# Attention scores of two heads as products in halves of the TensorE array, in a one-core hybrid encoder block

## The chip, the cores and the metric

The kernel runs on one core of one Trainium2 chip. The metric is the device time of one execution in microseconds (us); the time of a kernel is the median of several executions. TensorE (PE) multiplies matrices, VectorE (DVE), ScalarE (ACT) and GpSimd (POOL) do the work by elements, and SyncE (SP) issues most of the DMAs. A product reads a stationary operand, which a weight load (PEld in the profile) puts into the array first, and a moving operand, and writes into PSUM, which the kernel divides into eight banks of 128 partitions by 512 float32.

## What is computed

One encoder block over 1024 tokens of width 1024, in float32 accuracy:

```
h = rms_norm(x); [q|k|v|u] = h @ w_in
A: 8 heads x 64: 2-D neighbourhood attention on a 16 x 64 grid of tokens,
   window 8 rows x 16 columns, per-head RMS norm of q and k, relative-position bias
B: 4 groups x 128: centred mean pooling (windows 2, 4, 8, 16) minus the token,
   a linear map per group, a scale per channel
x = x + concat(A, B) @ w_out
x = x + (silu(h2 @ w_gate) * (h2 @ w_up)) @ w_down,  h2 = rms_norm(x)
```

For each query, attention takes the 8 x 16 keys of its window: scores times 1/8 plus bias, softmax, and the sum of the values.

## The kernel before

Every large product is made of three products of float32r operands: an operand is split into a high part (h) and the rest (l), and h*h, h*l and l*h are added in PSUM. `split` makes the parts: ACT writes h, DVE the rest. Tokens are ordered so that a tile of 64 queries is 4 rows by 16 columns, and a block of 128 keys is 4 rows by 32 columns.

Three stages follow one another. First the input projection of head pair 0, and the pooling branch. Then, for the four head pairs p, a stage in which attention is threaded between dense products (the projections of the next pairs, then `w_out`). Last the SwiGLU with its products of sums of blocks. The change touches the second stage.

There a unit is (p, b, Q): head pair p, one of four column strips b, one of four query tiles Q. 64 units. For each unit:

- `scores` (L561): the 64 queries of both heads lie as a block-diagonal 128 x 128 stationary operand (`qbd`, rows of head 0 against queries of head 0, rows of head 1 against those of head 1, zero elsewhere), so the output has head 0 on 64 partitions and head 1 on the other 64. The keys of two or three blocks are the moving operand: 256 or 384 columns (`QR`). Three products go into the one bank of the pool `ssp`. DVE adds the (negated) bias `nb` and takes the minimum (L581), ACT takes the exponential with its sum (L592), DVE the reciprocal (L594), POOL multiplies in place (L595).
- `transposes` (L600), `LAG` = 2 units later: two or three PE transposes into one of the two banks of the pool `ptp`, then a split into `pthl`.
- `values` (L611), one unit later: for each block of keys R, three products of the values with all the query tiles that see it, added in the bank of the pool `pop`; after the last, two ACT copies into `mixf`.

`spread_q` (L544) writes the block-diagonal operand of a strip from `qf`, half of the partitions at a time: four ACT copies and four POOL subtractions per strip. `load_bias` (L535) fetches `nb` and negates it on POOL, three times per head pair. `proj_evac_b` (L294) transposes the normalised q and k into a bank of `ptp`; ACT writes scaled q (`qf`), and `split` writes `kh` and `kl`.

The order on PE is the program's order in this stage (`pin`). `step(u)` issues scores of unit u, transposes of unit u-2 and values of unit u-3, and then `run` takes some dense pieces (`FIRST`, `CYC`, `WCYC`), each of three products. A scheduler with its own estimate of times orders the other engines; each works its queue in order. A pool hands out its banks in turn, and an allocation waits until the bank's last reader is done. Large tiles come from 45 slots of 4 KB per partition (`slot`), with the same rule.

Of the kernel before, what the change touches and what calls it, by code (L numbers as in the profile page):

```python
# [30 lines left out]
QR = [[0, 1], [0, 1, 2], [1, 2, 3], [2, 3]]  # L31
RQ = [[0, 1], [0, 1, 2], [1, 2, 3], [2, 3]]
BCOL = [0, 256, 256, 640]
BW = 896
LAG = 2
# [19 lines left out]
def hybrid_block(ctx, tc, xT, xt, w1, wu, rpbx, wpool, wout, wgu, wd, g2, sm, out):  # L55
# [7 lines left out]
    ssp = ctx.enter_context(tc.tile_pool(name="ssp", bufs=1, space=PSUM))  # L63
    ptp = ctx.enter_context(tc.tile_pool(name="ptp", bufs=2, space=PSUM))
# [150 lines left out]
    def proj_alloc(p):  # L215
        qf = slot(F32, f"qf_{p}")
# [4 lines left out]
        kT[p], qT[p], vn[p] = (kh, kl), qf, (vnh, vnl)  # L221
        for a in (qf, kh, kl, vnh[:, 0], vnl[:, 0]):
            touch(a)
# [70 lines left out]
    def proj_evac_b(p, tt, pool=ptp):  # L294
        (kh, kl), qf = kT[p], qT[p]
# [25 lines left out]
    def u_pool(up, hook):  # L321
# [10 lines left out]
        for half in range(2):  # L332
            ps = bank(ssp, f"rb_{half}")
# [30 lines left out]
        def u_win(g):  # L364
# [38 lines left out]
            for half in range(2):  # L403
                ps = bank((ssp, pop)[half], f"py_{g}_{half}")
# [31 lines left out]
    sq_ = ExitStack()  # L436
    qp = sq_.enter_context(tc.tile_pool(name="qp", bufs=1))
    qbd = []
    for i in range(2):
        pair = []  # L440
        for s in "hl":
            q_ = qp.tile([P, 4, 2, 64], F32R, name=f"qbd{s}{i}")
            nc.gpsimd.memset(q_.bitcast(F32), 0.0)
            pair.append(q_)
        qbd.append(pair)
# [5 lines left out]
    ps = bank(ptp, "warm_ps")  # L451
# [30 lines left out]
    pj = [bank(pl, f"pj_0_{t}") for t, pl in enumerate((mmp, mmp, mmp, mmp, ssp, pop, ptp, ptp))]  # L482
# [23 lines left out]
    def turn(tt):  # L506
        proj_evac_b(0, tt, (mmp, mmp, pop, ptp)[tt])
# [27 lines left out]
    def load_bias(p, b):  # L535
# [3 lines left out]
        nb = ap.tile([P, BW], F32, name=f"nb_{p}_{b}", tag="nb", bufs=2)  # L539
# [4 lines left out]
    def spread_q(p, b):  # L544
        qv = qT[p].rearrange("p (q b i) -> p q b i", q=4, b=4)
        bh, bl = qbd[b % 2]
        for qs in (slice(0, 2), slice(2, 4)):
            for j in range(2):
                pr = slice(64 * j, 64 * j + 64)
                nc.scalar.copy(bh[pr, qs, j, :], qv[pr, qs, b, :])  # L550
                nc.gpsimd.tensor_tensor(  # L551
                    out=bl[pr, qs, j, :],
                    in0=qv[pr, qs, b, :],
                    in1=bh[pr, qs, j, :].bitcast(F32),
                    op=ALU.subtract,
                )

    units = [(p, b, Q) for p in range(NPAIR) for b in range(4) for Q in range(4)]
    es, pos = {}, {}

    def scores(p, b, Q):  # L561
        kh, kl = (a.rearrange("p (r n) -> p r n", n=256) for a in kT[p])
        bh, bl = qbd[b % 2]
        nb = nbs[p, b]
        c0 = CG0[b] * 32
        rs = QR[Q]
        n = len(rs) * P
        ps = bank(ssp, f"s_{p}_{b}_{Q}")
        rsl = slice(rs[0], rs[-1] + 1)
        mm3(  # L570
            ps[:, :n],
            bh[:, Q].rearrange("p j i -> p (j i)"),
            bl[:, Q].rearrange("p j i -> p (j i)"),
            kh[:, rsl, c0 : c0 + P],
            kl[:, rsl, c0 : c0 + P],
            True,
            True,
        )
        e = tp.tile([P, 384], F32, name=f"e_{p}_{b}_{Q}", tag="e", bufs=4)
        m = tp.tile([P, 1], F32, name=f"m_{p}_{b}_{Q}", tag="m")  # L580
        nc.vector.tensor_tensor_reduce(  # L581
            out=e[:, :n],
            in0=ps[:, :n],
            in1=nb[:, BCOL[Q] : BCOL[Q] + n],
            scale=1.0,
            scalar=BIG,
            op0=ALU.add,
            op1=ALU.min,
            accum_out=m,
        )  # L590
        sm = tp.tile([P, 1], F32, name=f"sm_{p}_{b}_{Q}", tag="sm")
        nc.scalar.activation(e[:, :n], e[:, :n], AF.Exp, bias=m, scale=-1.0, accum_out=sm)  # L592
        r = tp.tile([P, 1], F32, name=f"r_{p}_{b}_{Q}", tag="r")
        nc.vector.reciprocal(r, sm)  # L594
        nc.gpsimd.tensor_scalar(  # L595
            out=e[:, :n], in0=e[:, :n], scalar1=r, scalar2=1.0, op0=ALU.mult, op1=ALU.mult
        )
        es[p, b, Q] = e

    def transposes(p, b, Q):  # L600
        e = es.pop((p, b, Q))
        rs = QR[Q]
        n = len(rs) * P
        pt = bank(ptp, f"pt_{p}_{b}_{Q}")
        for i in range(len(rs)):
            tr(pt[:, i * P : i * P + P], e[:, i * P : i * P + P], ident)
        at = [0, 1, 4, 7][Q]
        sel = slice(at, at + 2 * len(rs) - 1, 2)
        split(pthl[0][:, sel, :], pthl[1][:, sel, :], pt[:, :n].rearrange("p (r i) -> p r i", i=P))

    def values(p, b, R):  # L611
# [3 lines left out]
        q0 = RQ[R][0]  # L615
        nq = len(RQ[R])
# [4 lines left out]
        dst = po[:, q0 * P : (q0 + nq) * P]  # L621
        base = [0, 2, 5, 8][R]
        ph, pl = (a[:, base : base + nq, :].rearrange("p a i -> p (a i)") for a in pthl)
# [3 lines left out]
        if R == 3:  # L627
            mv = mixf[p].rearrange("p (q b i) -> p q b i", q=4, b=4)
            pv = po.rearrange("p (q j i) -> p q j i", q=4, j=2)
            for j in range(2):  # L630
                pr = slice(64 * j, 64 * j + 64)
                nc.scalar.copy(mv[pr, :, b, :], pv[pr, :, j, :])

    def step(u):
        if u < len(units):
            p, b, Q = units[u]
            if b == 0 and Q == 0:
                attn_alloc(p)
            nxt = units[u + 4 - Q] if u + 4 - Q < len(units) else None
            if nxt and Q == 1:  # L640
                load_bias(*nxt[:2])
            if nxt and Q == 2:
                spread_q(*nxt[:2])
            scores(p, b, Q)
        if 0 <= u - LAG < len(units):
            transposes(*units[u - LAG])
        if 0 <= u - LAG - 1 < len(units):
            p, b, Q = units[u - LAG - 1]
            for R in ((), (0,), (1,), (2, 3))[Q]:
                values(p, b, R)  # L650

# [193 lines left out]
    pthl = [ap.tile([P, 10, P], F32R, name=f"pt_{h}") for h in "hl"]  # L845
    load_bias(0, 0)
    spread_q(0, 0)
    for u in range(len(units) + LAG + 1):
        if u % 16 == 14:
            flush()  # L850
        step(u)
# [6 lines left out]
        elif u > W0:  # L858
            run(WCYC[min(u - W0 - 1, len(WCYC) - 1)])
    run(1000)  # L860
    pin = False
    sa.close()
    sq_.close()
# [20 lines left out]
    banks2 = (ptp, ptp, pop)  # L884
# [218 lines left out]
    ring = (mmp, mmp, ssp, mmp, mmp)  # L1103
# [24 lines left out]
    sets = ((mmp, mmp, mmp, mmp), (ptp, ssp, ptp, pop))  # L1128
# [181 lines left out]
def _bias_layout(np, rpb):  # L1310
# [3 lines left out]
    j, cg, rq, c8 = p // 64, p // 32 % 2, p // 8 % 4, p % 8  # L1314
    out = np.empty((NPAIR, 3, P, BW), rpb.dtype)
    for b, pat in ((0, 0), (1, 1), (3, 2)):
        for Q in (0, 1, 3):
            rs = QR[Q]
            n = np.arange(len(rs) * P)
            key_row = (rs[0] + n // P) * 4 + n // 8 % 4  # L1320
            key_col = (CG0[b] + n // 32 % 4) * 8 + n % 8
            row, col = 4 * Q + rq, 16 * b + 8 * cg + c8
# [4 lines left out]
            for pr in range(NPAIR):  # L1327
                out[pr, pat, :, BCOL[Q] : BCOL[Q] + n.size] = pad[(2 * pr + j)[:, None], ri, ci]
# [45 lines left out]
```

## Time and profile before

| | before |
|---|---|
| median of 3 runs | 1023.52 us (1022.57 to 1025.68) |
| profiled execution: time, span | 1024.31 us, 1022.4 us |
| PE, weight loads (share of the span) | 99%, 85% |
| DVE, ACT, POOL | 63%, 42%, 39% |
| mean granted TensorE clock | 0.997 |
| attention stage | about 107 to 325 us |

Busy time says how long an engine had work, not that the work set the end. A row of the timeline gives start, duration, engine, line, operation, and out<-in. Products are pipelined, so that a product's duration in a row is longer than what it keeps PE from the next one; the distance between two starts is the second. In a row of groups, the figures after the bar are busy time in us and the mean ns of one.

### The profile page before, as it was taken

What the parts mean: (1) busy time and instruction counts of PE and PEld (TensorE: products, weight loads), DVE (VectorE), ACT (ScalarE), POOL (GpSimd) and SP (SyncE); (2) the same over time, 40 slices, a digit from 0 to 9 for tenths busy, and PEclk for the clock granted to TensorE, in tenths of its full rate; (3) what the DMA queues carried; (4) which work ended last, traced back from release to release, by engine and by line L of the source; (5) the groups of instructions that cost most, each with busy time, mean ns of one, the idle gap of its engine ahead of it and who ended that gap; (6) DMA issues with size and microseconds to landing.
All of it is one profiled execution on the core that took longest, in us unless ns stands there. A gap on an engine that the chain in (4) does not pass through costs nothing.

```text
span 1022.4 us, 13679 instructions
## 1 busy us (share of the span) xinstructions
PE 1007.9 (99%) x4905; PEld 866.5 (85%) x4905; DVE 648.6 (63%) x1115; ACT 429.5 (42%) x876; POOL 400.5 (39%) x448
## 2 busy tenths in 40 slices
PE   9899999999999998999999999999999999999998
PEld 9888999999788887888888888888888888888887
DVE  5577666668652667856545546545562499988872
ACT  7542676667842335523333233233241354533400
POOL 1000333344731145468648658657644400000180
PEclk9999999999999999999999999999999999999999
DMA  9400413134511323133133133233216984373402
GB/s 355 175 16 1 127 53 107 50 119 163 180 42 42 144 83 93 53 112 136 72 124 114 72 123 113 74 123 113 78 78 224 350 277 150 102 244 114 134 32 93
DMA packets 50117, 124.12 MB, mean 121 GB/s; under 512 B 5312, under 2 KB 14272, under 8 KB 50048
## 3 DMA queue, kind: packets, MB, share of 16 engines
q1 hardware_dynamic: 43120, 98.85, 29.0%
q0 software_dynamic: 5632, 20.19, 5.3%
q10 hardware_dynamic: 1296, 4.20, 1.0%
q8 instruction: 39, 0.64, 0.3%
q14 instruction: 30, 0.25, 0.1%
HBM read 90.45 MB, written 28.57 MB: 116 GB/s over the span
## 4 chain that ended last, share of the span: by engine, by line
PE 93%; DVE 4%; ACT 1%; issue 1%; DMA 1%; POOL 0%; ACTq 0%; DVEq 0%; SPq 0%; POOLq 0%
PE pj L89 12%; PE z L89 12%; PE w L89 12%; PE x L89 11%; PE pw L89 7%; PE pc L89 6%; PE pa L89 6%; PE y L89 6%; PE pd L89 6%; PE pu L89 4%; PE pb L89 3%; PE po L89 3%; PE s L89 3%; PE pt L94 2%; PE qkt L94 1%
## 5 line engine op out<-in xcount | busy, mean ns | idle before, releaser
L89 PE MATMUL x<-b_h,w 128*128 128x512 f32 x352 | 116.5, 393 | 0.0
L89 PE MATMUL pw<-wo,mx 128*128 128x512 f32 x384 | 94.2, 396 | 0.3 <-DVE vnl L279 0.2
L89 PE MATMUL pj<-w1h,xh 128*128 128x384 f32 x256 | 87.2, 346 | 0.0
L89 PE MATMUL pj<-w1l,xh 128*128 128x384 f32 x256 | 84.6, 335 | 0.0
L89 PE MATMUL pj<-w1h,xl 128*128 128x384 f32 x256 | 83.7, 336 | 0.0
L89 PEld LDWEIGHTS pw<-wo,mx 128*128 128x128 f32 x384 | 70.8, 189 | 14.6 <-DVE x L776 0.5
L1300 POOL TENSOR_TENSOR x2r<-x2r,u 128x512 f32<-128x512 f32 x12 | 23.8, 2024 | 149.7 <-DVE u L1258 149.7
L89 PEld LDWEIGHTS x<-b_h,w 128*128 128x128 f32 x352 | 66.3, 189 | 13.7
L595 POOL TENSOR_SCALAR e<-e,r 128x256 f32<-128x256 f32 (+1 forms) x64 | 39.5, 618 | 75.8 <-DVE r L594 75.1
L89 PE MATMUL x<-b_l,w 128*128 128x512 f32 x176 | 68.9, 391 | 0.0
L1019 POOL TENSOR_TENSOR ur<-ur,gr 128x512 f32<-128x512 f32 x33 | 52.8, 1601 | 39.7 <-issue 22.0
L116 DVE TENSOR_TENSOR w_s<-sa,w_s 128x512 fp32r<-128x512 f32 x44 | 45.5, 1034 | 27.8 <-ACT w_s L115 27.7
L115 ACT CAST a_h<-raw_a 128x1024 fp32r<-128x1024 f32 (+1 forms) x42 | 41.0, 978 | 48.9 <-PE pc L89 13.8
L89 PE MATMUL z<-bt_h,w_s 128*128 128x512 f32 x176 | 57.9, 389 | 0.0
L89 PE MATMUL w<-b_h,w_s 128*128 128x512 f32 x176 | 57.8, 389 | 0.0
L89 PE MATMUL z<-bt_h,w 128*128 128x512 f32 x176 | 57.8, 389 | 0.0
L89 PE MATMUL y<-bt_h,w_s 128*128 128x512 f32 x176 | 57.8, 389 | 0.0
L89 PE MATMUL w<-bt_h,w_s 128*128 128x512 f32 x176 | 57.8, 389 | 0.0
L551 POOL TENSOR_TENSOR qbdl<-qf,qbdh 64x128 fp32r<-64x128 f32 x64 | 30.1, 471 | 64.6 <-ACT qbdh L550 56.2
L581 DVE CUSTOM_DVE_ANT_0 e<-s,nb 128x256 f32<-128x256 f32 (+1 forms) x64 | 31.1, 486 | 33.7 <-PE s L89 32.9
L116 DVE TENSOR_TENSOR a_l<-raw_a,a_h 128x1024 fp32r<-128x1024 f32 (+1 forms) x42 | 49.8, 1189 | 3.4 <-ACT a_h L115 3.1
L972 POOL TENSOR_TENSOR sa<-raw_g,raw_g 128x512 f32<-128x512 f32 x11 | 14.7, 1341 | 94.0 <-DMA raw_g<-in_wgu 81.8
(256 smaller groups left out, 2804.2 us busy)
## 6 DMA issues: line engine op xcount, KB each, us to landing
raw_a<-gsd SPq DMA_DIRECT2D x77, 256.0 KB, 3.6
raw_g<-in_wgu SPq DMA_DIRECT2D x22, 512.0 KB, 4.1
raw_u<-in_wgu SPq DMA_DIRECT2D x22, 512.0 KB, 4.1
gsd<-gr POOLq DMA_DIRECT2D x22, 512.0 KB, 4.0
raw_d<-in_wd SPq DMA_DIRECT2D x20, 512.0 KB, 4.3
raw_w<-in_w SPq DMA_DIRECT2D x15, 384.0 KB, 4.1
gsd<-ur POOLq DMA_DIRECT2D x11, 512.0 KB, 3.2
nb<-in_rpbx SPq DMA_DIRECT2D x12, 448.0 KB, 3.8
```

The costliest lines, as they stand in the source:

```text
L89: i = nc.tensor.matmul(*a, **k)
L94: i = nc.tensor.transpose(*a)
L115: keep(nc.scalar.copy(h, src))
L116: keepd(nc.vector.tensor_tensor(out=l, in0=src, in1=h.bitcast(F32), op=ALU.subtract))
L551: nc.gpsimd.tensor_tensor(out=bl[pr, qs, j, :], in0=qv[pr, qs, b, :], in1=bh[pr, qs, j, :].bitcast(F32), op=ALU.subtract,)
L581: nc.vector.tensor_tensor_reduce(out=e[:, :n], in0=ps[:, :n], in1=nb[:, BCOL[Q] : BCOL[Q] + n], scale=1.0, scalar=BIG, op0=ALU.add, op1=AL ...
L595: nc.gpsimd.tensor_scalar(out=e[:, :n], in0=e[:, :n], scalar1=r, scalar2=1.0, op0=ALU.mult, op1=ALU.mult)
L972: tt(out=s1, in0=r0[:, 1], in1=r1[:, 1], op=ALU.add)
L1019: eng.tensor_tensor(out=res[i][c][:, l], in0=src, in1=g, op=ALU.mult)
L1300: nc.gpsimd.tensor_tensor(out=q, in0=q, in1=U2[c], op=ALU.add)
```

## The change

A unit becomes (p, b, H): two query tiles at a time, 32 units. No block-diagonal queries are made. Instead `proj_evac_b` splits q into `qh` and `ql`, and a product takes 64 partitions (one head) of them, with 128 queries as its stationary columns, against 64 partitions of the keys, always three blocks (384 columns). The six products of a unit alternate between the two heads, which lie on partitions 0 to 63 and 64 to 127, and write to two banks. Scores, transposes and the transposes of q and k share a pool of three banks (`stp`) in place of `ssp` and `ptp`. `LAG` is 1 (larger) unit, the values come ahead of the dense pieces and the transposes, and the dense pieces of two former units stand between them. `nb` has 2 x 2 x 384 columns instead of 896, and `pthl` is laid out by key block, head and query.

```diff
-LAG = 2
+LAG = 1
-    ssp = ctx.enter_context(tc.tile_pool(name="ssp", bufs=1, space=PSUM))
-    ptp = ctx.enter_context(tc.tile_pool(name="ptp", bufs=2, space=PSUM))
+    stp = ctx.enter_context(tc.tile_pool(name="stp", bufs=3, space=PSUM))
...
 def proj_evac_b(p, tt, pool=stp):
-        keep(nc.scalar.activation(qf[:, c], pt[:, 0:256], AF.Copy, scale=qscale))
+        qo = [a.rearrange("p (h b q i) -> p h q b i", h=2, b=4, q=2)[:, tt // 2, tt % 2] for a in (qh, ql)]
+        qi = pt[:, 0:256].rearrange("p (b i) -> p b i", b=4)
+        keep(nc.scalar.activation(qo[0], qi, AF.Copy, scale=qscale))
+        keepd(nc.vector.scalar_tensor_tensor(out=qo[1], in0=qi, scalar=qscale,
+              in1=qo[0].bitcast(F32), op0=ALU.mult, op1=ALU.subtract))
         split(kh[:, c], kl[:, c], pt[:, 256:512])
...
-        nb = ap.tile([P, BW], F32, name=f"nb_{p}_{b}", tag="nb", bufs=2)
+        nb = ap.tile([P, 2, 2, 384], F32, name=f"nb_{p}_{b}", tag="nb", bufs=2)
...
-    def spread_q(p, b):
...
+    units = [(p, b, H) for p in range(NPAIR) for b in range(4) for H in range(2)]
+    def scores(p, b, H):
+        heads = [slice(64 * j, 64 * j + 64) for j in range(2)]
+        pss = [bank(stp, f"s_{p}_{b}_{H}_{j}") for j in range(2)]
+        for n, (x, y) in enumerate(((0, 0), (0, 1), (1, 0))):
+            for ps, js in zip(pss, heads):
+                mm(ps[:, :384], qv[x][js, H, b], kv[y][js, H : H + 3, c0 : c0 + P],
+                   start=n == 0, stop=n == 2)
+        for j, ps in enumerate(pss):
+            e = tp.tile([P, 384], F32, name=f"e_{p}_{b}_{H}_{j}", tag="e", bufs=4)
+            nc.vector.tensor_tensor_reduce(out=e, in0=ps[:, :384], in1=nb[:, H, j], ...)
+            nc.scalar.activation(e, e, AF.Exp, bias=m, scale=-1.0, accum_out=sm[:, j : j + 1])
+        nc.vector.reciprocal(r, sm)
+        for j, e in enumerate(es[p, b, H]):
+            nc.gpsimd.tensor_scalar(out=e, in0=e, scalar1=r[:, j : j + 1], ...)
+    def transposes(p, b, H):
+        pts = [bank(stp, f"pt_{p}_{b}_{H}_{j}") for j in range(2)]
+        for e, pt in zip(es[p, b, H], pts):
+            for i in range(3):
+                tr(pt[:, i * P : i * P + P], e[:, i * P : i * P + P], ident)
+        for j, pt in enumerate(pts):
+            h, l = (a[:, H : H + 3, j, P * H : P * H + P] for a in pthl)
+            split(h, l, pt[:, :384].rearrange("p (r i) -> p r i", i=P))
+    def step(v, more):
+        ... load_bias of the next strip at H == 0; scores(v)
+        if 0 <= v - LAG - 1 < len(units):
+            p, b, H = units[v - LAG - 1]
+            for R in ((0,), (1, 2, 3))[H]:
+                values(p, b, R)
+        more(2 * v)
+        if 0 <= v - LAG < len(units):
+            transposes(*units[v - LAG])
+        more(2 * v + 1)
```

`more(u)` holds the former choice of dense pieces for unit u. The other users of `ssp` and `ptp` (the first projections, the pooling branch, the SwiGLU) take `stp` instead; `BCOL`, `BW`, `QR`, `qbd` and its pool are gone; the bias array is laid out anew on the host side of the call.

More of the change, by code (lines that the diff above doesn't have):

```diff
@@ L434, in cook_wu @@
         cook(("wu", g), *wus[g])
[L436 to L445, printed above, removed]
     su = ExitStack()
@@ L450, in hybrid_block @@
     nc.vector.memset(warm.bitcast(F32), 0.0)
-    ps = bank(ptp, "warm_ps")
+    ps = bank(stp, "warm_ps")
     for _ in range(WARM):
@@ L481, in hybrid_block @@
     cook_wu(0)
-    pj = [bank(pl, f"pj_0_{t}") for t, pl in enumerate((mmp, mmp, mmp, mmp, ssp, pop, ptp, ptp))]
+    pj = [bank(pl, f"pj_0_{t}") for t, pl in enumerate((mmp, mmp, mmp, mmp, stp, pop, stp, stp))]
     pin = True
@@ L542, in load_bias @@
         nbs[p, b] = nb
-    def spread_q(p, b):
[L545 to L556, printed above, removed]
@@ L558, in hybrid_block @@
-    units = [(p, b, Q) for p in range(NPAIR) for b in range(4) for Q in range(4)]
+    units = [(p, b, H) for p in range(NPAIR) for b in range(4) for H in range(2)]
     es, pos = {}, {}
-    def scores(p, b, Q):
-        kh, kl = (a.rearrange("p (r n) -> p r n", n=256) for a in kT[p])
-        bh, bl = qbd[b % 2]
+    def scores(p, b, H):
+        kv = [a.rearrange("p (r n) -> p r n", n=256) for a in kT[p]]
+        qv = [a.rearrange("p (h b n) -> p h b n", h=2, b=4) for a in qT[p]]
         nb = nbs[p, b]
@@ L581, in scores @@
[L581 to L609, printed above, removed]
+        heads = [slice(64 * j, 64 * j + 64) for j in range(2)]
@@ new lines, in scores @@
+        es[p, b, H] = []
+        for j, ps in enumerate(pss):
+            e = tp.tile([P, 384], F32, name=f"e_{p}_{b}_{H}_{j}", tag="e", bufs=4)
+            m = tp.tile([P, 1], F32, name=f"m_{p}_{b}_{H}_{j}", tag="m", bufs=4)
+            nc.vector.tensor_tensor_reduce(
+                out=e,
+                in0=ps[:, :384],
+                in1=nb[:, H, j],
+                scale=1.0,
+                scalar=BIG,
+                op0=ALU.add,
+                op1=ALU.min,
+                accum_out=m,
+            )
+            nc.scalar.activation(e, e, AF.Exp, bias=m, scale=-1.0, accum_out=sm[:, j : j + 1])
+            es[p, b, H].append(e)
@@ L628, in values @@
             mv = mixf[p].rearrange("p (q b i) -> p q b i", q=4, b=4)
-            pv = po.rearrange("p (q j i) -> p q j i", q=4, j=2)
             for j in range(2):
                 pr = slice(64 * j, 64 * j + 64)
[L632 to L637, printed above, removed]
-                attn_alloc(p)
[L639 to L649, printed above, removed]
+                nc.scalar.copy(mv[pr, :, b, :], pv[pr, j].rearrange("p (q i) -> p q i", q=4))
+    def step(v, more):
+        if v < len(units):
+            p, b, H = units[v]
+            if b == 0 and H == 0:
+                attn_alloc(p)
+            if H == 0 and v + 2 < len(units):
+                load_bias(*units[v + 2][:2])
+            scores(p, b, H)
+        if 0 <= v - LAG - 1 < len(units):
+            p, b, H = units[v - LAG - 1]
+            for R in ((0,), (1, 2, 3))[H]:
                 values(p, b, R)
+        more(2 * v)
+        if 0 <= v - LAG < len(units):
+            transposes(*units[v - LAG])
+        more(2 * v + 1)
     late = []
@@ L844, in hybrid_block, with more @@
     tp = sa.enter_context(tc.tile_pool(name="tp", bufs=3))
-    pthl = [ap.tile([P, 10, P], F32R, name=f"pt_{h}") for h in "hl"]
+    pthl = [ap.tile([P, 4, 2, 256], F32R, name=f"pt_{h}") for h in "hl"]
     load_bias(0, 0)
[L847 to L851, printed above, removed]
+    def more(u):
         if u < 11:
@@ L859, in hybrid_block @@
             run(WCYC[min(u - W0 - 1, len(WCYC) - 1)])
+    for v in range(len(units) + LAG + 1):
+        if v % 8 == 7:
+            flush()
+        step(v, more)
     run(1000)
@@ L1313, in _bias_layout @@
     p = np.arange(P)
-    j, cg, rq, c8 = p // 64, p // 32 % 2, p // 8 % 4, p % 8
-    out = np.empty((NPAIR, 3, P, BW), rpb.dtype)
+    half, cg, rq, c8 = p // 64, p // 32 % 2, p // 8 % 4, p % 8
+    out = np.empty((NPAIR, 3, P, 2, 2, 384), rpb.dtype)
+    n = np.arange(384)
     for b, pat in ((0, 0), (1, 1), (3, 2)):
[L1317 to L1320, printed above, removed]
+        for H in range(2):
+            key_row = (H + n // P) * 4 + n // 8 % 4
             key_col = (CG0[b] + n // 32 % 4) * 8 + n % 8
-            row, col = 4 * Q + rq, 16 * b + 8 * cg + c8
+            row, col = 4 * (2 * H + half) + rq, 16 * b + 8 * cg + c8
             r0, c0 = np.clip(row - 4, 0, 8)[:, None], np.clip(col - 8, 0, 48)[:, None]
@@ L1327, in _bias_layout @@
             for pr in range(NPAIR):
-                out[pr, pat, :, BCOL[Q] : BCOL[Q] + n.size] = pad[(2 * pr + j)[:, None], ri, ci]
+                for j in range(2):
+                    out[pr, pat, :, H, j] = pad[2 * pr + j, ri, ci]
     return out
```

69 lines of the change are left out of this document (34 added, 35 removed).

## Prediction

> **What bounds the kernel now.** I read the page first (busy shares, then the chain that ended last), then the busy times by stretch, then the PE timeline inside the attention stage, then the groups by shape, then who waits.
>
> ```profile
> PE 1007.9 (99%) x4905; PEld 866.5 (85%) x4905; DVE 648.6 (63%) x1115; ACT 429.5 (42%) x876; POOL 400.5 (39%) x448
> PE 93%; DVE 4%; ACT 1%; issue 1%; DMA 1%; POOL 0%; ACTq 0%; DVEq 0%; SPq 0%; POOLq 0%
> ```
>
> PE works 99% of the span and carries 93% of the chain. In the attention stage (107 to 325 us) it is so too:
>
> ```profile
> core 0: us, PE busy (x) PEld busy (x) DVE busy (x) ACT busy (x) POOL busy (x), PEclk, DMA share, GB/s
> 107.00:260.00 153.00, 151.26 (x959) 148.91 (x960) 104.23 (x342) 106.71 (x319) 59.39 (x117) 1.00 0.33 100
> 260.00:325.00 65.00, 62.00 (x323) 52.90 (x322) 32.12 (x91) 33.00 (x90) 26.04 (x36) 0.97 0.25 85
> PE po L89 <- DVE pt_l L116: 1.9, 3, 1.2
> ```
>
> Up to 260 us PE is idle for 1.7 of 153 us; after it for 3.0 of 65, at a granted clock of 0.97 (another 65 x 0.03 = 2.0 us). The longest wait for a split of transposed probabilities is 1.2 us. So a microsecond of PE work added or removed in this stage is nearly a microsecond of the time, and work on DVE, ACT or POOL counts only where it delays PE.
>
> **Prices on PE.** The distance between starts is the price. Two stretches of the timeline hold one unit of each shape:
>
> ```profile
> 197.71 0.28 PE L89 MATMUL s<-kh,qbdh 128*128 128x256 f32 x1
> 197.83 0.28 PE L89 MATMUL s<-kl,qbdh 128*128 128x256 f32 x1
> 197.95 0.28 PE L89 MATMUL s<-kh,qbdl 128*128 128x256 f32 x1
> 198.07 0.49 PE L94 MATMUL pt<-ident,e 128*128 128x128 f32 x3
> 198.31 0.36 PE L89 MATMUL po<-pt_h,vsh 128*128 128x256 f32 x1
> 198.51 0.28 PE L89 MATMUL po<-pt_l,vsh 128*128 128x256 f32 x1
> ...
> 200.32 0.34 PE L89 MATMUL s<-kh,qbdh 128*128 128x384 f32 x1
> 200.50 0.34 PE L89 MATMUL s<-kl,qbdh 128*128 128x384 f32 x1
> 200.67 0.34 PE L89 MATMUL s<-kh,qbdl 128*128 128x384 f32 x1
> 200.84 0.38 PE L94 MATMUL pt<-ident,e 128*128 128x128 f32 x2
> 200.98 0.42 PE L89 MATMUL po<-pt_h,vsh 128*128 128x384 f32 x1
> 201.24 0.34 PE L89 MATMUL po<-pt_l,vsh 128*128 128x384 f32 x1
> ```
>
> Three products of 256 columns take 198.07 - 197.71 = 0.36 us (0.12 each), three of 384 take 0.52 (0.173 each). From the start of three transposes to the second product behind them is 0.44, less 0.12 for the first product 0.32: 0.107 each; for two, 0.40 - 0.173 = 0.227, 0.113 each. I take 0.11. Each has a weight load of its own, so a load of 128 columns can follow another within 0.11 us.
>
> ```profile
> L89 PE MATMUL s<-kh,qbdh x64: 279/336/522, 107.3 to 313.6; 128*128 128x256 f32 x32, 128*128 128x384 f32 x32
> L94 PE MATMUL pt<-ident,e x160: 270/272/417, 111.9 to 319.2; 128*128 128x128 f32 x160
> ```
>
> **Scores.** Before: 32 units of each shape, so 32 x (0.36 + 0.52) = 28.2 us. After: 32 larger units of six 384-column products on 64 rows each. No row of this trace shows a product on 64 rows, so I bound it. One after the other at 0.173: 32 x 1.04 = 33.2, +5.0 us. Two heads wholly side by side: 32 x 0.52 = 16.6, -11.6 us. Side by side, but paced by six weight loads of 128 columns at 0.11: 32 x 0.66 = 21.1, -7.1 us. I take -7.1: the number of loads does not fall, and the pitch of the transposes is the only row in which products shorter than a load show it.
> The Trainium skill, page TensorE: Matmul & The Clock Gate, section Part 3 (row/col tiling), says that products in different row groups start about 4 ns apart and run concurrently. By that alone the scores would save the 11.6 us; nothing in this trace shows it yet.
>
> **Changing between 64 and 128 rows.** Each of the 32 units goes into the halves and out again: 64 changes. Not shown before; the lower bound is 0 (the chain of transposes shows kinds of product changing without a total loss; a gain is excluded, since each change only adds a condition). Nearest rows: a first product behind transposes holds PE 0.20 instead of 0.12 (198.31 to 198.51), 0.08 extra, because its weight load isn't done ahead; and a 384-column product lasts 0.34 at a pitch of 0.173, a tail of 0.167 that a wait for the array to empty would expose. Tail and weight load together, 0.167 + 0.11 = 0.28, is the upper end. Ends: 0 and 64 x 0.28 = 17.9 us. I take the middle of the two nearest rows, 0.125: +8.0 us.
> The Trainium skill, page TensorEngine Tiling (Array Packing), section Key Properties, has it that a change of the tiling mode, as opposed to a change of tile, drains the array. By it the 64 changes would cost at least the tail, 64 x 0.167 = 10.7, and the sum would be +7.1 (1030.6); it speaks against this change, and no run here shows it so far.
>
> **Transposes.** 64 blocks of two or three become 32 of six: 160 become 192, 32 x 0.11 = +3.5 us.
>
> **Values** have the same columns (2 heads x 64 or 128 or 192 instead of 128 per tile), 0.
>
> **The other engines.** Every score row now has 384 columns, and spreading q goes.
>
> ```profile
> L581 DVE CUSTOM_DVE_ANT_0 e<-s,nb 128x384 f32<-128x384 f32 x32 | 17.7, 553 | 13.7 <-PE s L89 13.2
> L581 DVE CUSTOM_DVE_ANT_0 e<-s,nb 128x256 f32<-128x256 f32 x32 | 13.4, 420 | 20.1 <-PE s L89 19.7 <-issue 0.4
> L116 DVE TENSOR_TENSOR kl<-qkt,kh x16: 397/418/426, 41.6 to 259.4; 128x256 fp32r<-128x256 f32 x16
> L594 DVE RECIPROCAL r<-sm 128x1 f32<-128x1 f32 x64 | 10.2, 159 | 11.5 <-ACT e L592 10.6
> L550 ACT CAST qbdh<-qf 64x128 fp32r<-64x128 f32 x64 | 19.0, 296 | 15.0 <-PE s L89 14.2
> L551 POOL TENSOR_TENSOR qbdl<-qf,qbdh 64x128 fp32r<-64x128 f32 x64 | 30.1, 471 | 64.6 <-ACT qbdh L550 56.2 <-PE pt L94 6.0
> L541 POOL TENSOR_SCALAR nb<-nb 128x896 f32<-128x896 f32 x12 | 11.4, 948 | 33.0 <-DMA nb<-in_rpbx 33.0
> ```
>
> DVE: 32 bias additions grow by 0.133 (+4.3), 32 rests of the split likewise (estimate +4.3), 16 new rests `ql` at 0.42 like `kl` (+6.7), 32 reciprocals fewer (-5.1): +10 us on 136 in the stage's 218. ACT loses 19.0 of copies and gains some 7 us in longer exponentials and casts. POOL loses 30.1 and gains 11.4 x (1536/896 - 1) = 8.1 in `nb`, some 2 in the normalisation. All of it lies beside PE: priced 0 as work. If the cover of PE's 151 us goes, DVE with 104 + 7 of 153 is still far from being the bound.
>
> SP issues the same twelve `nb` transfers, 768 instead of 448 KB, one strip ahead instead of three quarters of one. POOL waits in its queue for each and the normalisations stand behind it; a strip is 218/16 = 13.6 us, so this is hidden: 0.
>
> **Waits that the three shared banks add.** The fourth allocation waits for the first. The second head's scores of unit v+1 take the bank of the first head's transposes of unit v-1 and so wait for their split; behind that product stands all of PE. Between lie three transposes (0.33), three to five dense pieces of three 0.173 products (1.6 to 2.6) and one product: 2.1 to 3.1 us. The split, three transposes from 198.07 on:
>
> ```profile
> 198.62 0.46 ACT L115 CAST pt_h<-pt 128x384 fp32r<-128x384 f32 x1
> 199.56 0.55 DVE L116 TENSOR_TENSOR pt_l<-pt,pt_h 128x384 fp32r<-128x384 f32 x1
> ```
>
> It ends at 200.11, 1.8 us after the last of them starts, so mostly in time. A transpose of q and k taken in between shifts the turn by a bank, onto the second split (another 0.6 us): I give these a microsecond in all. Against it, ACT and POOL become lighter just where PE idles (260 to 325): a microsecond back. Taken 0; ends -3 (that idle time gone) and +6 (0.2 us in each of 32 units).
>
> **The sum:** -7.1 + 8.0 + 3.5 + 0 = +4.4 us. The profiled execution took 1024.31 us (span 1022.4), 0.8 over the median of 1023.52; on the median, 1027.9, so 1028.0.
>
> **Rivals.**
> 1. Faster: changes between 64 and 128 rows are hidden by weight loads that are issued ahead, as all loads before a plain product are in the rows above. This case decides once a change costs under (7.1 - 3.5)/64 = 0.056 us. At 0 the sum is -3.6 (1020); with pairs at 0.173 instead of 0.22 it is -11.6 + 3.5 = -8.1 (1015.4). For it: going from scores to transposes shows no gap. Against: the 0.08 behind the transposes. Chance 0.38, of which the last form 0.14.
> 2. The halves don't overlap, because PE takes its products strictly in turn as it does in every row shown: +5.0 + 3.5 = +8.5, without any cost of change, 1032; with the forecast's cost 1040. Chance 0.13.
> 3. Overlap, but the full 0.28 at each change: -7.1 + 17.9 + 3.5 = +14.3, 1037.8. Chance 0.10.
> 4. The banks bind: +4.4 + 6 = 1034. Chance 0.07.
> The forecast itself has 0.32, single largest since rival 1 holds two times; its own range, with a change at 0.08 to 0.167, is 1024.6 to 1030.6.
>
> **Numbers.** About 0.3%, 3 us, is what a measurement of this kernel can tell from no change. Faster: 0.14 of the last form of rival 1, and 0.15 of its 0.24 else: 0.29. The same: the remaining 0.09 and 0.13 of the forecast (a change under 0.105): 0.22. Slower: 0.19 of the forecast and rivals 2 to 4: 0.49. The range from 1016 to 1038 leaves out the end of rival 1's last form (about 0.07) and of rivals 2 and 3 (about 0.10).
>
> **What would show it.** Starts of the two heads' products within some 0.05 us of each other, pairs 0.22 apart: overlap, paced by loads; 0.173 between all: none. The distance from a unit's last score product to the next product, over 0.173, and from the product before into the first: the cost of a change. 192 transposes at 0.11. Waits of `s` on `pt_l` above 0.2 us per unit: the banks. `qbd` rows gone, DVE about 10 us more. Wrong would be the forecast if the stage's PE starts show changes under 0.05 us, or if the difference lies outside 107 to 325 us.

## The result, and the profile after

| | before | after |
|---|---|---|
| median of 4 runs | 1023.16 us (1022.57 to 1025.68) | 1032.12 us (1031.04 to 1033.46) |
| ratio of the times | | 1.0083 (95%: 1.0061 to 1.0105) |
| profiled execution: time, span | 1024.31, 1022.4 us | 1031.04, 1029.2 us |

The change makes the kernel slower by 0.6 to 1.05%, about 8.5 us; in the two profiled executions the spans differ by 6.8 us. One execution of all that follow, of e7, took 1255.15 us at a granted clock of 0.753 and is left out of that kernel's median and ratio. The page and the busy times by stretch of the changed kernel (columns as in the prediction):

```profile
PE 1011.7 (98%) x4937; PEld 855.6 (83%) x4937; DVE 660.7 (64%) x1099; ACT 416.7 (40%) x812; POOL 375.3 (36%) x384
107.00:260.00 153.00, 147.82 (x936) 134.44 (x934) 103.00 (x311) 91.03 (x256) 41.28 (x72) 1.00 0.38 114
260.00:335.00 75.00, 72.90 (x385) 58.70 (x384) 40.39 (x102) 38.35 (x99) 23.52 (x28) 0.95 0.29 92
```

PE's busy time rose by 3.8 us over the span. Up to 260 us it is idle for 5.2 us instead of 1.7, with lighter ACT and POOL beside it. These rows show more waiting, but they don't show the larger part of the loss: a product's row lasts past the start of the next, so a gap of 0.1 us between two starts leaves no idle time in them. The starts show it. Here is one unit of scores in the timeline of the changed kernel (start, duration, engine; "x2" stands for both heads):

```profile
200.51 0.19 PEld L85 LDWEIGHTS pj<-w1h,xl 128*128 128x128 f32 x1
200.68 0.34 PE L85 MATMUL pj<-w1h,xl 128*128 128x384 f32 x1
...
200.94 0.19 PEld L85 LDWEIGHTS s<-kh,qh 64*128 64x128 f32 x2 [0.25 <-DVE ql L305]
200.94 0.45 PE L85 MATMUL s<-kh,qh 64*128 64x384 f32 x2
201.05 0.19 PEld L85 LDWEIGHTS s<-kl,qh 64*128 64x128 f32 x2
201.23 0.34 PE L85 MATMUL s<-kl,qh 64*128 64x384 f32 x2
...
201.40 0.35 PE L85 MATMUL s<-kh,ql 64*128 64x384 f32 x2
...
201.68 0.19 PEld L85 LDWEIGHTS po<-pt_h,vsh 128*128 128x128 f32 x1 [0.26 <-issue]
201.68 0.38 PE L85 MATMUL po<-pt_h,vsh 128*128 128x256 f32 x1
...
201.90 0.28 PE L85 MATMUL po<-pt_l,vsh 128*128 128x256 f32 x1
```

Two things are to be seen.

**The heads run wholly side by side.** Both products of a pair stand in one row (where both banks are free, their starts are mostly 3 to 4 ns apart), and from the second pair to the third it is 201.40 - 201.23 = 0.17 us, the price of a single 384-column product. Two weight loads in two halves cost no more than one.

**A change of rows holds PE twice.** Before a plain dense product the weight load starts with the product before it (200.51 for the product at 200.68). At the change it doesn't: the last full product begins at 200.68, and the first load on 64 rows only at 200.94, together with its product: 0.26 instead of 0.17. The bracket there names `ql`, but the load is late in all 32 units, by 0.09 to 0.10 in each, however long the last operation it needs had been done; so this is not a wait for `ql`. From this first pair to the next are 0.29 instead of 0.17, because its load wasn't done ahead. Leaving is alike: 0.28 from 201.40 to the values' load, and 0.22 instead of 0.12 for the first product of values. The four extras, 0.09 + 0.12 + 0.11 + 0.10, make 0.41 in this unit; the median of the 32 units is 0.40, and a whole unit keeps PE 0.925 us. That is 0.20 per change and 12.9 us in all, 32 times the unrounded 0.404.

The rows by tile, and the groups for the other engines:

```profile
L85 PE MATMUL s<-kh,qh x64: 421/440/444, 106.6 to 318.2; 64*128 64x384 f32 x64
L90 PE MATMUL pt<-ident,e x192: 270/272/417, 113.6 to 328.2; 128*128 128x128 f32 x192
L305 DVE SCALAR_TENSOR_TENSOR ql<-qkt,qscale,qh 128x256 fp32r<-128x256 f32 x16 | 7.6, 477 | 5.2 <-ACT qh L303 5.2
```

And who waits on PE:

```profile
PE qkt L90 <- DVE qn L260: 4.4, 3, 2.5
PE pt L90 <- DVE kl L112: 2.6, 2, 1.3
...
PE s L85 <- DVE pt_l L112: 1.3, 1, 1.3
```

Transposes of probabilities now wait for `kl`, the last split of a bank that held transposed q and k: 2.6 us in two places. Before, no such row stood among the waits. At one of the two places the split is late after ACT has taken the cast of a large weight ahead of `kh`:

```profile
202.20 0.83 ACT L111 CAST w1h<-raw_w 128x768 fp32r<-128x768 f32 x1 [1.75 <-DMA raw_w<-in_w]
202.94 0.36 ACT L111 CAST kh<-qkt 128x256 fp32r<-128x256 f32 x1
203.07 0.96 DVE L112 TENSOR_TENSOR w1l<-raw_w,w1h 128x768 fp32r<-128x768 f32 x1 [1.18 <-ACT w1h L111]
204.61 0.41 DVE L112 TENSOR_TENSOR kl<-qkt,kh 128x256 fp32r<-128x256 f32 x1
205.17 0.99 PE L90 MATMUL pt<-ident,e 128*128 128x128 f32 x6 [1.27 <-DVE kl L112]
```

The wait of `s` for `pt_l` is listed once, since only there PE ran dry. The starts show it in six units: the second head's first product stands 0.15 to 1.70 us behind the first head's (near 117, 151, 208, 250, 278 and 292 us), each time 0.04 us after a `pt_l` is done, and the six units take 2.8 us more in all than the usual 0.925. The longest of them:

```profile
278.02 0.44 PE L85 MATMUL s<-kh,qh 64*128 64x384 f32 x1
279.72 0.44 PE L85 MATMUL s<-kh,qh 64*128 64x384 f32 x1 [1.26 <-DVE pt_l L112]
```

**The sum as measured**, each product counted at the distance of its kind in both traces: scores -11.6, changes +12.9, transposes +3.5; together PE's work grows by 4.8 us. To set this against the right time, take the stage from the first product of scores to the last of `w_out` (first and last start in the rows, first before, then after):

```profile
L89 PE MATMUL pw<-wo,mx x384: 387/389/628, 252.6 to 375.6; 128*128 128x512 f32 x192
L85 PE MATMUL pw<-wo,mx x384: 388/389/628, 260.9 to 384.4; 128*128 128x512 f32 x192
```

It takes 268.3 us before (107.3 to 375.6) and 277.8 after (106.6 to 384.4): 9.5 more. Ahead of the stage 0.7 us are won and behind it 2.0, where the kernel before runs at half clock for 3.4 us from 396 us on and the changed one doesn't; so the spans differ by 6.8 only. Of the 9.5, PE's work is 4.8, a second stretch at half clock inside the stage (two instead of one, see the last section) 1.7, and the remaining 3 us are more waiting. The medians lie further apart than the profiled executions, since that of before took 1.2 us more than its median and that of after 1.1 us less: two of the four runs after had a mean granted clock of 0.997 (1031.04, 1031.38 us) and two of 0.993 (1032.86, 1033.46).

### The profile page after: what moved, and what is told of

It is laid out like the page before. It is cut to its first block, busy times and chain, and to the rows that moved or that the text cites. A ratio compares the mean times of both kernels' runs of the same rounds, so it can differ in the third digit from the quotient of the medians.

```text
span 1029.2 us, 13513 instructions
## 1 busy us (share of the span) xinstructions
PE 1011.7 (98%) x4937; PEld 855.6 (83%) x4937; DVE 660.7 (64%) x1099; ACT 416.7 (40%) x812; POOL 375.3 (36%) x384
## 4 chain that ended last, share of the span: by engine, by line
PE 90%; DMA 5%; DVE 3%; ACT 1%; issue 1%; SPq 0%; DVEq 0%; ACTq 0%
PE x L85 12%; PE w L85 12%; PE z L85 12%; PE pj L85 8%; PE pw L85 8%; PE y L85 6%; PE pc L85 6%; PE pa L85 6%; PE pd L85 6%; PE pu L85 4%; PE pb L85 3%; PE po L85 3%; DMA raw_w<-in_w 2%; PE s L85 2%; PE pt L90 2%; DMA raw_xt<-in_xt 1%
## 5 line engine op out<-in xcount | busy, mean ns | idle before, releaser
L577 POOL TENSOR_SCALAR e<-e,r 128x384 f32<-128x384 f32 x64 | 37.6, 599 | 102.6 <-DVE r L575 82.8
L112 DVE TENSOR_TENSOR w_s<-sa,w_s 128x512 fp32r<-128x512 f32 x44 | 45.1, 1026 | 29.2 <-ACT w_s L111 29.0
L573 ACT ACTIVATE e<-e,m 128x384 f32<-128x384 f32 x64 | 39.0, 611 | 32.5 <-DVE m L563 31.9
L112 DVE TENSOR_TENSOR pt_l<-pt,pt_h 128x384 fp32r<-128x384 f32 x64 | 33.6, 551 | 27.9 <-ACT pt_h L111 27.9
L85 PEld LDWEIGHTS pj<-w1h,xh 128*128 128x128 f32 x256 | 47.9, 188 | 2.2 <-ACT xh L171 1.6
```

Source lines behind the costliest of these rows:

```text
L85: i = nc.tensor.matmul(*a, **k)
L112: keepd(nc.vector.tensor_tensor(out=l, in0=src, in1=h.bitcast(F32), op=ALU.subtract))
L573: nc.scalar.activation(e, e, AF.Exp, bias=m, scale=-1.0, accum_out=sm[:, j : j + 1])
L577: nc.gpsimd.tensor_scalar(out=e, in0=e, scalar1=r[:, j : j + 1], scalar2=1.0, op0=ALU.mult, op1=ALU.mult)
```

## The experiments

Two theories at first. **Theory 1**: the changes of rows eat what the pairs save; the rest is small. **Theory 2**, the rival: a change is nearly free over a whole unit, and the time is lost in waits (shared banks, a heavier DVE). **Theory 3** came with the later runs: one slot more per head pair, for `ql`, holds up what else takes slots. Ratios are to the kernel before; the changed kernel stands at 1.0083.

**e1, full rows.** Three products on 128 rows in the first bank and one in the second, all else as changed. It leaves the heads unseparated, so its scores aren't attention scores; what counts is that PE never changes its rows and that every engine behind gets the same shapes.

```diff
-            for ps, js in zip(pss, heads):
-                mm(ps[:, :384], qv[x][js, H, b], kv[y][js, H : H + 3, c0 : c0 + P], ...)
+            mm(pss[0][:, :384], qv[x][:, H, b], kv[y][:, H : H + 3, c0 : c0 + P], ...)
+        mm(pss[1][:, :384], qv[0][:, H, b], kv[0][:, H : H + 3, c0 : c0 + P], start=True, stop=True)
```

> The changed kernel with the scores as products on all 128 rows, so that PE never changes between 64 and 128 rows: three passes of 384 columns into the first head's bank and one into the second's, banks and everything behind them as they were. It leaves out the separation of the two heads and two of the passes of the second. Theory 1 (each change between 64 and 128 rows costs PE 0.20 us, 0.09 of waiting and a weight load of 0.107 that isn't done ahead; in the changed kernel's profile a score block costs 0.926 us where three pairs at 0.174 would be 0.52): a block is 4 x 0.174 = 0.70, 32 x 0.226 = 7.2 us less than the changed kernel, about 1025 us. Theory 2 (the changes are cheap or stand where PE would wait in any case, and what was lost are waits for the three shared banks and for a fuller DVE queue): a product more per unit, 32 x 0.174 = 5.6 us more, about 1037.5 us.

Measured: 1021.34 us, 0.9969 (0.9955 to 0.9983); profiled span 1021.6, 7.6 below the changed kernel's. PE's timeline:

```profile
199.16 0.33 PE L85 MATMUL pj<-w1h,xl 128*128 128x384 f32 x1
199.34 0.33 PE L85 MATMUL s<-kh,qh 128*128 128x384 f32 x1
199.51 0.33 PE L85 MATMUL s<-kl,qh 128*128 128x384 f32 x1
199.68 0.33 PE L85 MATMUL s<-kh,ql 128*128 128x384 f32 x1
199.86 0.33 PE L85 MATMUL s<-kh,qh 128*128 128x384 f32 x1
200.03 0.28 PE L85 MATMUL po<-pt_h,vsh 128*128 128x256 f32 x1
```

Four full products take 0.69 us (0.70 in the median), less than three pairs with their changes (0.925); no start is late on either side. 32 x (0.925 - 0.70) = 7.1 us. The stage, taken as above, lasts 265.9 us here (108.7 to 374.6), 11.9 less than in the changed kernel: 7.1 from the starts, 1.7 because one stretch at half clock in it is missing, and some 3 us of waits. With the same banks, and the same work on the other engines, this kernel waits no more than the kernel before: its stage is 2.4 us shorter than that one's, and PE's work alone gives 32 x (0.70 - 0.88) + 3.5 = -2.3. So the waits that the changed kernel has gained are not the price of the shared banks by themselves; why they come up with it is not shown. (The spans differ by 7.6 only, since the profiled execution of e1, one of its two slowest, is at half clock for 3.4 us ahead of the stage, near 42 us, and for 6.8 us behind it, near 395; the medians differ by 11.) A cost that lies in the waits alone would have left this kernel slower than the changed one, by one product in each unit, 32 x 0.17; that is refuted.

**e2, twice the changes.** The values stand between a unit's first pair and the other two, so that it goes into the halves twice; the work is the same.

```diff
             for ps, js in zip(pss, heads):
                 mm(ps[:, :384], qv[x][js, H, b], ...)
+            if n == 0:
+                between()          # the values of the unit two steps back
```

> The changed kernel with the value products of the older unit placed behind the first of the three pairs of score products and not behind the last, so that PE goes into the halves and out again twice per unit; the same products in all. Theory 1: 30 units x 2 more changes x 0.20 = 12 us more than the changed kernel, about 1044 us. Theory 2: within 2 us of it, about 1032 us.

Measured: 1045.31 us, 1.0202 (1.0183 to 1.0220), 12 to 13 us above the changed kernel. 30 units have two changes more; by the starts such a unit takes 1.315 us in its two parts instead of 0.925, 30 x 0.39 = 11.7 us, or 0.2 for each further change, and the stage is 11.6 us longer (289.4, 108.8 to 398.2). In PE's timeline the extras return at each visit, 0.27 in, 0.37 for the lone pair, 0.28 for the product behind it:

```profile
199.15 0.34 PE L85 MATMUL pj<-w1h,xl 128*128 128x384 f32 x1
199.42 0.45 PE L85 MATMUL s<-kh,qh 64*128 64x384 f32 x2
199.79 0.44 PE L85 MATMUL po<-pt_h,vsh 128*128 128x384 f32 x1
200.07 0.34 PE L85 MATMUL po<-pt_l,vsh 128*128 128x384 f32 x1
...
201.38 0.45 PE L85 MATMUL s<-kl,qh 64*128 64x384 f32 x2
...
201.94 0.44 PE L85 MATMUL pj<-w1h,xh 128*128 128x384 f32 x1
```

Without changes the extras are gone, and with twice as many they are there twice: a change has the same price from both sides.

**e3, heads in turn.** Three products of the first head, then three of the second, to see whether the overlap needs the alternating order.

```diff
-        for n, (x, y) in enumerate(((0, 0), (0, 1), (1, 0))):
-            for ps, js in zip(pss, heads):
+        for ps, js in zip(pss, heads):
+            for n, (x, y) in enumerate(((0, 0), (0, 1), (1, 0))):
```

> The changed kernel with the three products of the first head ahead of the three of the second, not in turns. If products of the two halves run side by side only where they are neighbours in PE's order, one of three pairs is left and a block costs 5 x 0.174 + 0.40 = 1.27 instead of 0.926 us: 11 us more, about 1043 us. The rival, that PE takes the other half's products ahead of their turn: no change, about 1032 us.

Measured: 1035.56 us, 1.0115 (1.0097 to 1.0134). PE's timeline:

```profile
201.80 0.45 PE L85 MATMUL s<-kh,qh 64*128 64x384 f32 x2
202.08 0.35 PE L85 MATMUL s<-kl,qh 64*128 64x384 f32 x2
202.26 0.35 PE L85 MATMUL s<-kh,ql 64*128 64x384 f32 x2
202.54 0.38 PE L85 MATMUL po<-pt_h,vsh 128*128 128x256 f32 x1
```

The pairs are there, 10 to 19 ns between the heads' starts, though the first head's three come first in PE's program; the median unit takes 0.937 us. So the order doesn't matter for the overlap where both banks are free, and the second head's first product started before the first head's second. The further 3 us aren't in such units: in the profiled execution PE is at half clock for five times 3.4 us instead of two (below), and the waits are longer, `s` for `pt_l` among them with 3.5 us instead of 1.3.

**e4, q and k from SBUF.** To give the bank of transposed q and k back sooner, two ACT copies empty it, and POOL makes the four splits from the copies.

```diff
+        qs, ks = (tq.tile([P, 256], F32, name=f"{n}s_{p}_{tt}", tag="sq", bufs=2) for n in "qk")
+        nc.scalar.activation(qs, pt[:, 0:256], AF.Copy, scale=qscale)
+        nc.scalar.copy(ks, pt[:, 256:512])
+        nc.gpsimd.tensor_copy(qo[0], qi)
+        nc.gpsimd.tensor_tensor(out=qo[1], in0=qi, in1=qo[0].bitcast(F32), op=ALU.subtract)
+        ... and the same two for kh and kl
```

> The changed kernel with the transposed q and k of head pairs 1 to 3 brought out of their shared bank by two ACT copies alone; both parts of each are then made on POOL from SBUF. That takes 12 x (0.48 + 0.41) = 10.7 us from DVE and the bank no longer waits for kl on DVE, for which PE waited 1.5 and 1.4 us in the profile (near 147 and 204 us). Theory 1 (the changes and the transposes carry the loss, the banks are the small rest): 1 to 3 us less than the changed kernel, 1029 to 1031 us. Theory 2 (banks and DVE queue carry it): at least half of the 8.5 us lost comes back, 1028 us or less.

Measured: 1040.58 us, 1.0161 (1.0143 to 1.0180), 8 us slower than the changed kernel; no theory had that. One new wait is the largest of PE's, and the rows ahead of it show a part of what made it late:

```profile
263.80 1.48 POOL L545 TENSOR_SCALAR nb<-nb 128x1536 f32<-128x1536 f32 x1
264.03 1.26 DVE L98 TENSOR_TENSOR rsq_q<-y 128x8 f32<-128x8 f32 x1
265.22 0.40 POOL L318 CAST kh<-ks 128x256 fp32r<-128x256 f32 x1
265.32 0.32 DVE L99 SCALAR_TENSOR_TENSOR rsq_q<-rsq_q,v 128x8 f32<-128x8 f32 x1
265.58 0.73 POOL L317 TENSOR_TENSOR ql<-qs,qh 128x256 fp32r<-128x256 f32 x1
265.68 0.66 DVE L100 SCALAR_TENSOR_TENSOR y<-rsq_q,y 128x8 f32<-128x8 f32 x1
...
267.63 0.79 PE L85 MATMUL pw<-wo,mx 128*128 128x512 f32 x1 [5.39 <-DVE vnl L276]
```

Three DVE instructions on eight columns each end within 0.05 us of the end of the POOL instruction beside them (265.29 and 265.28, 265.64 and 265.62, 266.34 and 266.31). The first stands beside `nb`, which the changed kernel computes as well; the other two stand beside POOL's new work, which thus lengthened DVE's chain to `qn` and `vnl` by some 0.6 us at this place. Of the 8 us, 3.4 are clock: PE is at half clock for 6.8 us from 266 us on and again from 280 us on, where the changed kernel has 3.4 us twice. Why the rest of the 5.4 us came up was not taken apart.

**e5, one block per strip.** Both halves H of a strip together: 16 blocks of twelve products, 32 changes instead of 64, with the values' bank put into the shared pool (four banks). Transposes and values follow by strips too, and the bias has one buffer instead of two.

```diff
-    stp = ctx.enter_context(tc.tile_pool(name="stp", bufs=3, space=PSUM))
-    pop = ctx.enter_context(tc.tile_pool(name="pop", bufs=1, space=PSUM))
+    stp = ctx.enter_context(tc.tile_pool(name="stp", bufs=4, space=PSUM))
+    pop = stp
...
+    def scores(p, b):
+        both = [products(p, b, H) for H in range(2)]
```

> The changed kernel with the scores of both units of a strip in one block: 16 blocks of twelve products on 64 rows, so 32 changes between 64 and 128 rows in place of 64. For the four banks that this takes, the values' bank joins the shared pool (four banks for scores, transposes and values); transposes and values follow by strips too, the bias has one buffer and the exponentials eight. Theory 1 (a change costs 0.20 us): 32 x 0.20 = 6.4 us less than the changed kernel, about 1025 to 1026 us, and 1 to 3 us more or less by the other waits. Rival (the number of products, not of changes): no gain, about 1032 us.

Measured: 1032.33 us, 1.0080 (1.0065 to 1.0095): no gain on the changed kernel. Eight of the sixteen blocks (not nine, as the expectation of e10 below has it) run 1.45 us without a stop, six pairs and one visit's 0.41, so the saving of 16 x 0.40 = 6.4 us on changes is there. The other eight stop inside the block until a bank comes free, 0.57 to 3.1 us from one product to the next, and together take some 13 us more than eight times 1.45 (one of them partly at half clock). One of them in PE's timeline, where the second head's first product comes 0.93 us after the first head's:

```profile
176.14 0.34 PE L85 MATMUL s<-kh,qh 64*128 64x384 f32 x1
177.07 0.44 PE L85 MATMUL s<-kh,qh 64*128 64x384 f32 x1 [0.59 <-DVE m L571]
```

And the two longest waits of this kind among those of PE:

```profile
PE s L85 <- ACT mixf L618: 2.8, 1, 2.8
PE s L85 <- DVE kl L112: 2.8, 3, 1.3
```

A block that needs four banks waits for the slowest reader of any. The saving was turned into these waits; which of the edit's parts brings them, the larger block, the shared bank of the values or the other order, was not separated.

**e10 and e11** try to get it back. e10 is e5 with the transposes of q and k moved to one place per strip; e11 is e10 with `qh` and `ql` of head pairs 1 to 3 made on POOL, from an ACT copy.

```diff
-                proj_evac_b(p, t // 2 - 1)
+                late.append((p, t // 2 - 1))     # and flush(2) behind the transposes of a strip
```

> The kernel with one block per strip, with the transposes of q and k put off to one place per strip, right behind the transposes of the probabilities, so that their bank comes free long before the next block. In the profile of the kernel with one block per strip, 9 of 16 blocks run their twelve products without a stop (1.45 us each) and 7 stop in the middle for a bank, for about 10 us in all. Theory 1 with these stops as what hid its gain: half of them or more go, 4 to 6 us less than that kernel, 1026 to 1028 us on the scale on which the changed kernel has 1032. Rival (the stops only move): within 2 us of 1032.

> As the kernel before in this list, with the parts of q of head pairs 1 to 3 made on POOL from a small SBUF tile of its own that one ACT copy fills, so that DVE loses 12 x 0.48 = 5.7 us and the bank waits for one operation less. If DVE's extra operation is what cost the changed kernel 3.8 us (as leaving it out showed): another 2 to 4 us less, 1023 to 1026 us, about the time of the kernel before the change. Rival (work on POOL comes back on DVE's path as when q and k were both made there): no gain or a loss.

Measured: 1032.58 us, 1.0086 (1.0071 to 1.0101), and 1031.40, 1.0071 (1.0058 to 1.0084). Neither gains clearly: both intervals hold the changed kernel's 1.0083, and e11 misses the 1023 to 1026 us that were expected of it. In e10, 14 of 16 blocks run without a stop, but the stops moved to where q and k are transposed, as PE's waits show:

```profile
PE qkt L90 <- DVE pt_l L112: 6.7, 8, 2.2
```

**e7, no `ql`.** The third pass reads `qh` again; neither the DVE instruction nor the slot is there, and q's low part is left out.
**e8, `ql` into a scratch tile.** The instruction is done, the slot isn't taken, the third pass reads `qh`.
**e13, the slot kept and zeroed, no instruction**; q's low part is left out except for POOL's zeroing.

```diff
-        ql = slot(F32R, f"ql_{p}")
+        ql = qh                                   # e7 and e8
...
-        keepd(nc.vector.scalar_tensor_tensor(out=qo[1], in0=qi, ...))      # e7 and e13; in e8 out is a scratch tile
```

> The changed kernel without the rest of q: no tile ql (one 4 KB slot less per head pair) and no DVE operation that makes it; the third pass of the scores takes qh again, so the products are as many. Theory 3 (beside the changes of rows, the loss comes from the 45 slots: qh and ql in place of one qf take one more per pair, the last two fetches of w_in for the next pair wait longer for a slot, ACT and DVE stand behind them, and PE waits 1.5 and 1.4 us for the bank that kl holds): 3 to 5 us less than the changed kernel, about 1027 to 1029 us. Rival (these waits are only where the scheduler happened to put them): within 2 us of the changed kernel.

> As the kernel without ql, but the DVE operation that makes the rest of q is kept and writes to a small scratch tile, so that only the slot is saved. If the slot counts: within 1.5 us of the kernel without ql (1027 to 1029 us). If the DVE operation counts: as the changed kernel, about 1032 us.

> The changed kernel without the DVE operation that makes the rest of q, but with the slot of ql kept: POOL fills it with zeros once per head pair, the third pass reads the zeros, and the rest of q is left out of the scores. Leaving out slot and operation took 3.8 us from the changed kernel, leaving out the slot alone nothing, and moving the operation to POOL nothing. If the DVE operation by itself is the cause, and POOL's work gave its gain back: 1028 to 1029 us. If the gain needed slot and operation together, or was only a luckier order of the queues: about 1032 us.

Measured: e7 1028.25 us, 1.0046 (1.0030 to 1.0063); e8 1033.70, 1.0094 (1.0079 to 1.0110); e13 1031.26, 1.0070 (1.0057 to 1.0084). Without instruction and slot 3.8 us come back, by the ratios. Without the slot alone nothing does. Without the instruction alone it is 1.3, and by the two intervals anything from none to all of e7's gain. In the profiled execution of e7 the stage is 3.2 us shorter than in the changed kernel, and 1.7 of that is one stretch at half clock instead of two. So the slot alone isn't the cause; whether the instruction is, or the two together, or POOL's zeroing hides a part in e13, stays open.

**e12, `ql` on POOL.** The changed kernel, q split on POOL for head pairs 1 to 3.

```diff
+        if p:
+            qs = tq.tile([P, 256], F32, name=f"qs_{p}_{tt}", tag="qs", bufs=1)
+            nc.scalar.activation(qs, pt[:, 0:256], AF.Copy, scale=qscale)
+            nc.gpsimd.tensor_copy(qo[0], qv_)
+            nc.gpsimd.tensor_tensor(out=qo[1], in0=qv_, in1=qo[0].bitcast(F32), op=ALU.subtract)
```

> The changed kernel with the parts of q of head pairs 1 to 3 made on POOL from a small SBUF tile of its own, nothing else: the DVE operation goes, and nothing is left out of the computation. If DVE's queue carries that part of the loss: 2 to 4 us less than the changed kernel, 1028 to 1030 us. If it is not DVE's queue: within 1.5 us of it, or slower as when q and k both went over POOL (1040 us).

Measured: 1032.64 us, 1.0084 (1.0071 to 1.0097). DVE is rid of the instruction in twelve of sixteen places and nothing is gained: waits for `qn` stand at 5.2 us instead of 4.4, and a new one of `po` for `pt_h` at 2.0. If DVE's work is what e7 took away, POOL isn't the place to put it.

**e9, before with 44 slots.** For theory 3, the other way round: the kernel before with one slot fewer.

```diff
-SLOTS = 45
+SLOTS = 44
```

> The kernel before with 44 slots in place of 45, nothing else. Theory 3: the fetches of w_in come later here too, 2 to 4 us slower than the kernel before (1025 to 1027.5 us). Rival (slots are not short): within 1 us of it.

Measured: 1022.70 us, 0.9990 (0.9981 to 0.9999). Slots aren't short in the kernel before; with e8 theory 3 falls.

No version that computes the whole beat the kernel before by more than its measurement can tell.

## Why the prediction was right, and where its sizes were off

It had +4.4 us and "slower" as the likeliest. The profiled executions show +6.8 (+9.5 in the stage itself, so the loss lies where it was forecast), the comparison of all runs 8.5. By its steps:

- **What bounds the stage** held in the main: 4.8 of the 9.5 us in the stage are PE's own work. e2 moves the stage by what it moves on PE (11.7 against 11.6), e1 by more (7.1 against 11.9, with the clock and the waits as above).
- **Scores, -7.1: mis-sized, -11.6 measured.** The pace of 0.11 per weight load was taken from transposes on all 128 rows. In the halves two loads go side by side, and pairs are 0.17 apart instead of 0.22. The prediction named this value as its bound, but gave it a chance (0.14) only together with changes that cost nearly nothing. That products in different row groups run together, as the Trainium skill says (page TensorE: Matmul & The Clock Gate, section Part 3), the trace shows, with mostly 3 to 4 ns between the heads' starts; that loads do so as well stands in the Trainium skill's page TensorEngine Tiling (Array Packing), section Key Properties, and agrees with the 0.17. The Trainium skill's page TensorE: Matmul & The Clock Gate, section Part 3, also has products start strictly in program order; e3, where the second head's first product starts 0.27 us ahead of the first head's second, which precedes it in the program, differs.
- **Changes, +8.0: mis-sized, +12.9 measured.** The price was the middle of two rows (0.08 and 0.167), and the first was misread. The product behind transposes holds PE 0.08 longer, but the last transpose ahead of it only 0.03 (three that start 0.108 apart from 198.07 on, so the third near 198.28, and the product at 198.31): 0.23 together, as much as 0.11 and 0.12, so there is no extra. The prediction's own 0.11 per transpose had that 0.08 in it already. What a change costs is two terms one behind the other: 0.09 to 0.11 until the load may start, and 0.10 to 0.12 for the load that wasn't done ahead. The prediction's upper end, 0.28, had both, with too long a first part; its own range should begin at 1025.0 by its terms, not 1024.6. The Trainium skill's rule that a change of tiling mode drains the array (page TensorEngine Tiling (Array Packing), section Key Properties) agrees in kind, since the load waits at every change; the wait is 0.09 to 0.11, shorter than the tail of 0.167 that the estimate took for it.
- **The two errors cancel**: scores and changes together +0.9 predicted, +1.3 measured. That these two came out near in sum was luck, a wrong split of a right total, and only the starts show that.
- **Transposes, +3.5**: 192 instead of 160, with rows of 0.27 us as before and 0.11 from start to start; right.
- **Other engines, 0**: DVE rose by 12.1 us over the span and by 8.2 in the stage (the prediction had +10, with `ql` at 6.7 where 7.6 was measured). As plain work it lies beside PE. But e7 gives back 3.8 us with `ql` gone, so "hidden" may be too simple for it; how, is not shown.
- **Waits, 0: mis-sized, some +3, and +1.7 of clock behind them.** The second head's products do wait for `pt_l`, as the prediction described, but in six units only, 2.8 us in all or 0.09 per unit; `pt` waits for `kl`, on a bank of q and k, another 2.6. The prediction gave both "a microsecond in all" and set it off against a gain from lighter ACT and POOL that did not come. In return PE's earlier waits, such as 1.9 us of `po` for `pt_l`, became shorter (0.5), so that the sum is less than the parts. e1, which has the same banks and loses nothing by them, shows that the number of banks alone does not explain it.
- **Rivals**: 1 falls (a change costs 0.20, its limit was 0.056). 2 falls (the halves overlap). 3 had the right kind of cost at a too high price. 4, with 6 us of such waits, is at most a part here, but in e5, where a block needs four banks, the waits for them use up what the changes save.

## What to carry to other kernels

Count a visit to the halves of the array at its fixed price: here it cost 0.40 us, and three pairs, 0.52 us in place of 0.88 of full products, saved only 0.36; the more products stand in one visit, the better it pays. Read such a cost from the distances between starts on both sides of the change, since busy shares don't show it. Before merging blocks to save changes, count the banks that the larger block holds at once and who reads them last.

## What the runs showed of the hardware that was not expected

- Where nothing has to be waited for, the two halves take their products independently of the order in which the program mixes them (e3: starts 10 to 19 ns apart), and their weight loads run side by side. A product that waits does hold up the other half's products behind it in the program: at 279.72 us of the changed kernel the first head's second product starts 4 ns after the late one of the second head, 1.70 us after the first head's first.
- After waits of PE that are shorter than 3 us the granted clock can fall to half for 3.4 us. In the changed kernel PE waits 2.5 us for `qn` ahead of 258.99; then, in stretches of 2 us (the granted clock is the third figure from the end):

```profile
258.00:260.00 2.00, 1.01 (x8) 0.74 (x10) 2.00 (x10) 1.25 (x4) 0.00 (x0) 1.00 0.98 401
260.00:262.00 2.00, 2.00 (x12) 1.55 (x11) 2.00 (x7) 1.62 (x5) 1.09 (x1) 0.73 0.03 12
262.00:264.00 2.00, 2.00 (x7) 1.50 (x7) 1.20 (x6) 1.04 (x4) 0.97 (x3) 0.50 0.63 162
264.00:266.00 2.00, 2.00 (x12) 1.69 (x11) 1.19 (x3) 1.71 (x4) 0.56 (x1) 0.92 0.74 190
```

  The loss is 2 x (0.27 + 0.50 + 0.08) = 1.7 us, so the stretch lasts 3.4. The profiled execution has a second one from 281.4 on, behind waits of 0.51 us (ended at 274.18) and 1.26 (at 279.72), while single waits of 1.3 us near 147 and 204 us have none. That of before has two as well, one of them behind the stage, and e3 five times this length; so a wait on PE can cost more than its own length, and how many such stretches a run gets moves its time by a microsecond or two. What decides it is not shown.
- Small DVE instructions that ran beside a POOL instruction often ended when that one did (e4): 0.66 us for L100, which takes 0.15 to 0.17 in all its sixteen places in the changed kernel.
